# Tying a quad's differences to an earlier low part, and moving layer A's probability products one sub-block on

## The chip, the cores and the metric

The kernel runs on one core of one Trainium2 chip. The metric is the device time of one execution in microseconds (us). Five engines matter: PE (TensorE, matmuls), ACT (ScalarE), DVE (VectorE), POOL (GpSimd) and SP (SyncE, which here only issues transfers). Each works through its own queue in order, and they wait for each other through semaphores.

## The reference, cut to what matters

There are 256 tokens, a model width of 2048, an inner width of 4096, 32 heads of 128, one layer of each kind. All data are float32.

```python
h = rms_norm(x, a_norm)                                   # layer A
q, k, v, g = jnp.split(h @ a_w_in, 4, axis=-1)            # 2048 -> 4 * 4096
o = chunked_relbias_attention(q, k, v, a_rel_bias)        # softmax(q k^T * scale + bias) v, per head
x = x + (o * jax.nn.silu(g)) @ a_w_out                    # 4096 -> 2048
h_kv = rms_norm(x, kv_norm)                               # shared keys and values
k_sh, v_sh = jnp.split(h_kv @ kv_w, 2, axis=-1)
h = rms_norm(x, b_norm)                                   # layer B
q, g = jnp.split(h @ b_w_in, 2, axis=-1)
o = forgetting_attention(q, k_sh, v_sh, cum_log_f)        # softmax with a decay per key, causal
x = x + (o * jax.nn.silu(g)) @ b_w_out
return rms_norm(x, final_norm)
```

## The kernel before, in words

**Products.** A float32 product is made of three matmuls of rounded parts: with x = xh + xl and w = hi + lo, the kernel adds xh·hi, xh·lo and xl·hi. The weights stream in. A *sub-block* is 256 rows by 512 columns of a weight matrix (512 KB); SP loads it into a `raw` tile (6 buffers), ACT copies it, rounded, into `hi`, and DVE subtracts `lo = raw - hi` (hi and lo: 4 buffers each). PE then runs 12 matmuls on it (2 blocks of 128 rows, 2 halves of the tokens, 3 parts), each 128x512. `Feed.prepare` issues a sub-block's hi and lo up to `DEPTH` ahead of PE; `feed.by_act` and `feed.by_dve` remember the last of each.

**Units and pairs.** Layer A works on pairs of heads, g = 0 to 15. A pair has two *units* of 512 columns: `aqk` (q and k) and `avg` (v and gate), 8 sub-blocks each, each unit with two accumulators in PSUM (`aqk_acc`, `avg_acc`, one for each half of the tokens). For g > 0 the last two sub-blocks of both units are done together as *quads*: a 2x2 block product with seven products where there were eight (21 matmuls where there were 24). The order on PE in such a pair is: aqk 0 to 5; avg 0, 1; first quad; avg 2; second quad; avg 3, 4, 5 (`QUADS_A = (1, 2)` are the places of the quads behind avg's sub-blocks).

**A quad's operands.** `Quad.split(i)` makes four pairs of hi and lo from the raw sub-blocks `one` (of aqk) and `two` (of avg). i = 0 takes `one` as it stands; i = 1 takes the differences `t` (two subtractions, lines 299 and 300, into a tile that is named `first` in layer A); i = 2 takes half of `two`; i = 3 takes `one` again, overwritten by two more differences (lines 308 and 309, which come behind i = 0). So the rows are: ACT `quad_hi` (L305), DVE `quad_lo` (L306), DVE `first` (L299, L300), DVE `aqk_raw<-...` (L308, L309).

**Attention beside it.** The attention of the pair before runs as a generator (`side_a`, `attention`), whose steps are taken at places of the pair by tables: `A1_STEPS` counts behind aqk's sub-blocks, `A2_STEPS` behind avg's. Its steps: evacuate q and k (`qk`, L726, which also frees `aqk_acc`), transpose them on DVE (L519, into `first`) and through 16 small transfers into `sums` (8 on SP, 8 on POOL, L522); split them (`wide`, `q`); scores (`s1p`, `s0p` on PE); softmax; transpose the probabilities and the gate (`sgY` to `sgZ`, again 16 small transfers); split the probabilities (`wide<-sgZ`); multiply them with v (`op` on PE: six matmuls by `dot3`, L549 to L551, and two in plain float32, L613); then `oT` (L617). In the table before, the products `op` are issued behind avg 4.

**Order on the engines.** The program is written in one order; a scheduler then sets each engine's queue by what it expects to be ready. `tc.issue_after(ins)` holds what a block issues behind `ins` on the same engine.

**Output projection.** After layer A, `project(oA, ao, ...)` runs four units `ao0` to `ao3` over 16 sub-blocks with quads of their own (`ao_quads.order(first, second, n, lead)`: `lead` sub-blocks come ahead of the first quad), and the attention of pair 15 beside them by a list of counts. Layer B's pairs have one quad each; its output projection `bo` has five.

Of the kernel before, what the change touches and what calls it, by code (L numbers as in the profile page):

```python
# [30 lines left out]
KD = D // P  # L31
# [5 lines left out]
KB = 2  # L37
# [15 lines left out]
QUADS = 5  # L53
# [3 lines left out]
QUADS_A = (1, 2)  # L57
QUADS_B = (2,)
A1_STEPS = {3: 1, 4: 2}
A2_STEPS = {0: 1, 3: 1, 4: 99}  # L60
B1_STEPS = {3: 1, 5: 1, 6: 2}
B2_STEPS = {1: 1}
OLD_B_STEPS = {0: 1, 2: 99}
# [3 lines left out]
def r32(ap):  # L67
    return ap.bitcast(F32)
# [8 lines left out]
def trunk(ctx, tc, x, x_t, gains, a_w_in, a_rel, a_w_out, kv_w, f_w, f_b, b_w_in, b_w_out, final_norm, out):  # L77
    nc = tc.nc
    pe, act, dve, pool, sp = nc.tensor, nc.scalar, nc.vector, nc.gpsimd, nc.sync
# [50 lines left out]
    class Stat:  # L130
        def __init__(self, name, n):
            self.hi = [big_tile([P, BIG, S], F32R, name=f"{name}h{i}") for i in range(n // BIG)]
            self.lo = [big_tile([P, BIG, S], F32R, name=f"{name}l{i}") for i in range(n // BIG)]
# [55 lines left out]
    class Feed:  # L189
# [3 lines left out]
        def __init__(self, todo):  # L193
            self.todo = iter(todo)
            self.ready, self.loaded = [], []
            self.also, self.early = {}, []

        def buffer(self, name):
            return self.early.pop(0) if self.early else stream.tile([P, KB, IL, HN], F32, name=name, tag="raw",
# [21 lines left out]
        def prepare(self, ahead=True, parts=(slice(None),)):  # L221
            if not self.loaded:
                self.begin()
            if not self.loaded:
                return
            spec, b, raw, (before, behind) = self.loaded.pop(0)
            if not spec:
                self.ready.append(b[0].split(b[1]))
                self.refill()
                return  # L230
            if before:
                before()
            nm, h = spec["name"], b - (spec["nk"] // KB - spec["late"])
            if 0 <= h < spec["kept"]:
                both = big_tile([P, 2, KB, IL, HN], F32R, f"{nm}_keep{b}")
                hi, lo = both[:, 0], both[:, 1]
            else:
                hi = stream.tile([P, KB, IL, HN], F32R, name=f"{nm}_hi{b}", tag="hi", bufs=SPLIT)
                lo = stream.tile([P, KB, IL, HN], F32R, name=f"{nm}_lo{b}", tag="lo", bufs=SPLIT)
            if spec["g0"] is not None:  # L240
                for j in range(KB):
                    gk = gain[:, spec["g0"] + b * KB + j:][:, :1]
                    self.by_act = act.activation(hi[:, j], raw[:, j], AF.Copy, scale=gk)  # L243
                    self.by_dve = dve.scalar_tensor_tensor(lo[:, j], raw[:, j], gk, r32(hi[:, j]),  # L244
                                                           op0=OP.mult, op1=OP.subtract)
                parts = ()
            for j in parts:
                self.by_act = act.activation(hi[:, j], raw[:, j], AF.Copy)  # L248
                self.by_dve = dve.tensor_sub(lo[:, j], raw[:, j], r32(hi[:, j]))  # L249
            if behind:  # L250
                behind()
            self.ready.append((hi, lo))
            if ahead:
                self.refill()
# [26 lines left out]

    class Quad:

        def __init__(self, all_, specs, b, first, last):
            self.all, self.specs, self.b, self.first, self.last = all_, specs, b, first, last

        def split(self, i):

            one, two = self.raw
            t = self.all.t[:, 0]  # L290
            if not i:
                if self.specs[0]["g0"] is not None:
                    with tc.issue_after(feed.by_act.ins):
                        for raw, sp_ in zip(self.raw, self.specs):
                            for j in range(KB):
                                gk = gain[:, sp_["g0"] + self.b * KB + j:][:, :1]
                                act.activation(raw[:, j], raw[:, j], AF.Copy, scale=gk)
                with tc.issue_after(feed.by_dve.ins):
                    dve.tensor_sub(t[:, 0], two[:, 0], one[:, 0])  # L299
                    dve.tensor_sub(t[:, 1], two[:, 1], two[:, 0])  # L300
            src = [one, t, two[:, 1:], one][i]
            n = src.shape[1]
            hi = stream.tile([P, KB, IL, HN], F32R, name=f"quad_hi{i}", tag="hi", bufs=SPLIT)
            lo = stream.tile([P, KB, IL, HN], F32R, name=f"quad_lo{i}", tag="lo", bufs=SPLIT)
            feed.by_act = act.activation(hi[:, :n], src, AF.Copy)  # L305
            feed.by_dve = dve.tensor_sub(lo[:, :n], src, r32(hi[:, :n]))  # L306
            if not i:
                dve.tensor_sub(one[:, 0], two[:, 1], t[:, 0])  # L308
                dve.tensor_sub(one[:, 1], one[:, 1], one[:, 0])  # L309
            return hi, lo  # L310

        def step(self, lhs, first, second):
# [102 lines left out]
    a_quads = Quads("a")  # L415

    def paired(specs, places):

        n = len(places)
        quads = [Quad(a_quads, specs, KD // KB - n + i, not i, i == n - 1) for i in range(n)]  # L420
        todo.extend(whole(specs[0]))
        for i, item in enumerate(whole(specs[1])):
            todo.append(item)
            todo.extend((None, quads[k]) for k in range(n) if places[k] == i)
        return quads

    a_pairs = [paired(qkvg[2 * g:2 * g + 2], QUADS_A) for g in range(1, NG)]
    ao = [spec(f"ao{u}", a_w_out[u], KI) for u in range(4)]
    ao_quads, bo_quads = Quads("ao"), Quads("bo")
    ao_order = ao_quads.order(ao[0], ao[1], 3, 13) + ao_quads.order(ao[2], ao[3], QUADS, 4)  # L430
    todo += ao_order
    for g in range(NG):
        qkvg.append(spec(f"bqg{g}", b_w_in[g], KD, g0=GB, quads=len(QUADS_B) * (g > 0)))
# [8 lines left out]
    feed = Feed(todo)  # L442
# [36 lines left out]
    def project(lhs, specs, order, begun, closed, sides):  # L479


        units = {}

        def get(u):
            if u not in units:
                units[u] = Unit(lhs, specs[u])
            return units[u]

        for sp_, b in order:
            if sp_:  # L490
                us = [int(sp_["name"][-1])]
                get(us[0]).step(b)
            else:
                us = [int(u["name"][-1]) for u in b.specs]
                b.step(lhs, *(get(u) for u in us))
            for u in us:
                begun(u, units[u].left)
            for side, steps in sides:
                if steps:
                    steps[0] -= 1  # L500
                    while steps and steps[0] <= 0:
                        next(side, None)
                        steps.pop(0)
            for u in us:
                if not units[u].left:
                    more = closed(u, units[u].acc)
                    if more:
                        sides.append(more)
        for side, _ in sides:
            finish(side)  # L510
# [340 lines left out]
                           accum_out=ssq1[:, t, u:u + 1])  # L851
        return more and (more, [8, 7, 1, 1, 1] if u % 2 else [11, 1, 1, 1])

    project(oA, ao, ao_order, ao_begun, ao_closed, [(prev, [4, 1, 0, 1, 4, 1, 1]), (ao_quads.open(oA, QUADS), [3, 1, 1, 2, 26])])
    tot1 = const.tile([P, NT], F32, name="tot1")
    dve.tensor_reduce(tot1, ssq1, axis=AX.X, op=OP.add)
    rsB, halfB = rstd_of(tot1, "b")
# [236 lines left out]
```

## Time and profile before

| | |
|---|---|
| median of 3 runs | 1755.87 us (1755.2 to 1756.09) |
| the profiled execution's own time | 1756.25 us |
| its span | 1754.5 us |
| PE, DVE, ACT, POOL busy | 1721.5, 1560.7, 1200.3, 300.7 us |
| DMA, mean | 226 GB/s |

The span is what lies between the first and the last instruction; the rest of the execution's time, 1.75 us, lies around it. "Busy" counts an instruction's whole duration. PE's matmuls overlap: one of 128x512 lasts 0.38 us in the records, and the next may start long before it ends. So the time that PE loses at a wait is read from the starts of its matmuls, not from the idle time in a row.

A row of the timeline is: start in us, duration in us, engine, line, operation, output<-inputs, shape, and in brackets the idle time before it and what ended that.

### The profile page before, as it was taken

To read this page: it belongs to the slowest core of one execution; us is meant where nothing else is said; L and a number is where in the kernel's file an instruction comes from. 1 tells how busy PE (TensorE), PEld (TensorE's weight loads), DVE (VectorE), ACT (ScalarE), POOL (GpSimd) and SP (SyncE) were. 2 spreads that over 40 slices of the span, in tenths; PEclk is the share of its full clock that TensorE was granted. 3 is DMA by queue.
4 is the path that set the end of the run, shared out by engine and by line. 5 is a ranking of instruction groups with operands and counts; after the bars stand their busy time and mean duration, and the time that the engine had idled before them with its cause. 6 is when DMAs were issued, how large, how long until landed. Compare 5 with 4: busy or idle time off the path is not lost.

```text
span 1754.5 us, 27007 instructions
## 1 busy us (share of the span) xinstructions
PE 1721.5 (98%) x8213; PEld 1499.6 (85%) x8213; DVE 1560.7 (89%) x2378; ACT 1200.3 (68%) x2115; POOL 300.7 (17%) x623
## 2 busy tenths in 40 slices
PE   9999999999999999999999999999999999999997
PEld 7888888888888888888888888888888888888886
DVE  8799999999989999988977999999999989997887
ACT  7666666666656666655567777778788878775554
POOL 1011111111111111101121222212222122221000
PEclk9999999999999999999999999999999999999999
DMA  8666666666666666667775666666666666767654
GB/s 305 210 223 223 222 224 213 226 224 221 222 202 232 216 230 223 227 219 236 253 235 182 227 228 230 231 235 231 227 236 234 236 229 224 253 227 259 226 195 144
DMA packets 150321, 396.44 MB, mean 226 GB/s; under 512 B 31104, under 2 KB 51872, under 8 KB 150048
## 3 DMA queue, kind: packets, MB, share of 16 engines
q1 hardware_dynamic: 131536, 373.16, 61.1%
q0 software_dynamic: 17920, 20.48, 4.5%
q8 instruction: 66, 1.08, 0.3%
q10 hardware_dynamic: 720, 1.07, 0.2%
q14 instruction: 79, 0.65, 0.1%
HBM read 351.05 MB, written 4.23 MB: 202 GB/s over the span
## 4 chain that ended last, share of the span: by engine, by line
PE 84%; DVE 6%; DMA 5%; issue 2%; ACT 2%; SPq 0%; ACTq 0%; POOL 0%; DVEq 0%
PE bkv_acc L185 17%; PE bqg_acc L185 17%; PE aqk_acc L185 13%; PE avg_acc L185 9%; PE bo_acc L185 8%; PE ao_acc L185 6%; PE p L550 2%; PE p L551 2%; PE p L549 2%; DVE avg_lo L249 2%; DMA aqk_raw<-in_a_w_in 2%; DMA avg_raw<-in_a_w_in 1%; ACT quad_hi L305 1%; PE op L613 1%; DVE quad_lo L306 1%
## 5 line engine op out<-in xcount | busy, mean ns | idle before, releaser
L522 POOL DMA_DIRECT2D sums<-first x256 | 125.8, 499 | 563.0 <-ACT aqk_hi L248 254.4
L243 ACT ACTIVATE bqg_hi<-bqg_raw,gain 128x512 fp32r<-128x512 f32 x226 | 149.5, 713 | 85.4 <-DMA bqg_raw<-in_b_w_in 33.7
L244 DVE SCALAR_TENSOR_TENSOR bkv_lo<-bkv_raw,gain,bkv_hi 128x512 fp32r<-128x512 f32 x226 | 161.4, 761 | 16.4 <-ACT bkv_hi L243 16.2
L185 PE MATMUL bkv_acc<-bkv_hi,x1Th 128*128 128x512 f32 x452 | 167.7, 383 | 0.0
L185 PE MATMUL bqg_acc<-bqg_hi,x1Th 128*128 128x512 f32 x452 | 167.6, 382 | 0.0
L185 PE MATMUL bkv_acc<-bkv_hi,x1Tl 128*128 128x512 f32 x452 | 166.3, 380 | 0.0
L185 PE MATMUL bqg_acc<-bqg_hi,x1Tl 128*128 128x512 f32 x452 | 166.3, 380 | 0.0
L185 PE MATMUL bqg_acc<-bqg_lo,x1Th 128*128 128x512 f32 x452 | 166.3, 380 | 0.0
L185 PE MATMUL bkv_acc<-bkv_lo,x1Th 128*128 128x512 f32 x452 | 166.3, 380 | 0.0
L244 DVE SCALAR_TENSOR_TENSOR bqg_lo<-bqg_raw,gain,bqg_hi 128x512 fp32r<-128x512 f32 x226 | 156.4, 743 | 4.9 <-ACT bqg_hi L243 4.9
L243 ACT ACTIVATE bkv_hi<-bkv_raw,gain 128x512 fp32r<-128x512 f32 x226 | 145.1, 711 | 21.9 <-issue 14.7
L522 POOL DMA_DIRECT2D sgZ<-sgY x256 | 125.5, 498 | 155.1 <-PE avg_acc L185 80.1
L248 ACT ACTIVATE aqk_hi<-aqk_raw 128x1024 fp32r<-128x1024 f32 x95 | 100.3, 1056 | 70.6 <-PE avg_acc L185 47.4
L185 PE MATMUL aqk_acc<-aqk_hi,xTh 128*128 128x512 f32 x392 | 145.7, 385 | 0.0
L185 PE MATMUL avg_acc<-avg_hi,xTl 128*128 128x512 f32 x392 | 144.8, 383 | 0.0
L185 PE MATMUL aqk_acc<-aqk_lo,xTh 128*128 128x512 f32 x392 | 143.7, 380 | 1.0 <-DVE aqk_lo L249 1.0
L185 PE MATMUL avg_acc<-avg_lo,xTh 128*128 128x512 f32 x392 | 144.4, 382 | 0.0
L185 PE MATMUL aqk_acc<-aqk_hi,xTl 128*128 128x512 f32 x392 | 143.7, 380 | 0.0
L185 PE MATMUL avg_acc<-avg_hi,xTh 128*128 128x512 f32 x392 | 143.7, 380 | 0.0
L249 DVE TENSOR_TENSOR avg_lo<-avg_raw,avg_hi 128x1024 fp32r<-128x1024 f32 x97 | 115.9, 1222 | 11.7 <-ACT avg_hi L248 10.8
L248 ACT ACTIVATE avg_hi<-avg_raw 128x1024 fp32r<-128x1024 f32 x97 | 98.8, 1049 | 32.4 <-PE aqk_acc L185 28.0
L249 DVE TENSOR_TENSOR aqk_lo<-aqk_raw,aqk_hi 128x1024 fp32r<-128x1024 f32 x95 | 114.5, 1218 | 5.3 <-ACT aqk_hi L248 5.3
(373 smaller groups left out, 4614.0 us busy)
## 6 DMA issues: line engine op xcount, KB each, us to landing
bqg_raw<-in_b_w_in SPq DMA_DIRECT2D x128, 512.0 KB, 5.1
bkv_raw<-in_kv_w SPq DMA_DIRECT2D x128, 512.0 KB, 4.7
avg_raw<-in_a_w_in SPq DMA_DIRECT2D x127, 512.0 KB, 4.6
aqk_raw<-in_a_w_in SPq DMA_DIRECT2D x125, 512.0 KB, 5.3
ao_raw<-in_a_w_out SPq DMA_DIRECT2D x64, 512.0 KB, 4.5
bo_raw<-in_b_w_out SPq DMA_DIRECT2D x64, 512.0 KB, 4.3
sgZ<-sgY SPq DMA_DIRECT2D x256, 40.0 KB, 2.1
sgZ<-sgY POOLq DMA_DIRECT2D x256, 40.0 KB, 1.9
```

The costliest lines, as they stand in the source:

```text
L185: pe.matmul(acc[t], x[:, t * P:(t + 1) * P], w, start=t not in begun, stop=last and i == 2)
L243: self.by_act = act.activation(hi[:, j], raw[:, j], AF.Copy, scale=gk)
L244: self.by_dve = dve.scalar_tensor_tensor(lo[:, j], raw[:, j], gk, r32(hi[:, j]), op0=OP.mult, op1=OP.subtract)
L248: self.by_act = act.activation(hi[:, j], raw[:, j], AF.Copy)
L249: self.by_dve = dve.tensor_sub(lo[:, j], raw[:, j], r32(hi[:, j]))
L305: feed.by_act = act.activation(hi[:, :n], src, AF.Copy)
L306: feed.by_dve = dve.tensor_sub(lo[:, :n], src, r32(hi[:, :n]))
L522: queues[j].dma_start(out=r32(z)[j * SQ:(j + 1) * SQ, i], in_=y[i * SQ:(i + 1) * SQ, j])
L549: pe.matmul(out_, a[0], b[0], start=start, stop=False)
L550: pe.matmul(out_, a[0], b[1], start=False, stop=False)
L551: pe.matmul(out_, a[1], b[0], start=False, stop=stop)
L613: pe.matmul(op[:, i, 1::NT], v1[:, i * DH:(i + 1) * DH], pT[:, i, NT], start=False, stop=i == HG - 1)
```

## The change

Four things are edited.

1. Each low part is remembered in a list `lows`. The differences `t` of a quad (L299, L300) were held behind the latest low part; now they are held behind `lows[tie - 1]`. `tie` is 0 for first quads (and for all of ao, bo and layer B): the latest, as before. It is -2 for the second quad of a pair of layer A: the third last.
2. The low part of i = 1 is held behind the second overwriting difference (`self.ready`), in every quad.
3. `op` and what follows it is issued behind avg 5 instead of avg 4.
4. In the output projection, 14 sub-blocks instead of 13 come ahead of the first quad, and pair 15's `op` is issued one count later.

```diff
-A2_STEPS = {0: 1, 3: 1, 4: 99}
+A2_STEPS = {0: 1, 3: 1, 5: 99}
...
-            self.also, self.early = {}, []
+            self.also, self.early, self.lows = {}, [], []
...
                 self.by_dve = dve.tensor_sub(lo[:, j], raw[:, j], r32(hi[:, j]))
+            self.lows.append(self.by_dve)
...
-        def __init__(self, all_, specs, b, first, last):
+        def __init__(self, all_, specs, b, first, last, tie=0):
...
-                with tc.issue_after(feed.by_dve.ins):
+                with tc.issue_after(feed.lows[self.tie - 1].ins):
                     dve.tensor_sub(t[:, 0], two[:, 0], one[:, 0])
                     dve.tensor_sub(t[:, 1], two[:, 1], two[:, 0])
...
-            feed.by_dve = dve.tensor_sub(lo[:, :n], src, r32(hi[:, :n]))
+            with tc.issue_after(self.ready.ins) if i == 1 else nullcontext():
+                feed.by_dve = dve.tensor_sub(lo[:, :n], src, r32(hi[:, :n]))
+            feed.lows.append(feed.by_dve)
             if not i:
                 dve.tensor_sub(one[:, 0], two[:, 1], t[:, 0])
-                dve.tensor_sub(one[:, 1], one[:, 1], one[:, 0])
+                self.ready = dve.tensor_sub(one[:, 1], one[:, 1], one[:, 0])
...
-        quads = [Quad(a_quads, specs, KD // KB - n + i, not i, i == n - 1) for i in range(n)]
+        quads = [Quad(a_quads, specs, KD // KB - n + i, not i, i == n - 1, -2 * (i > 0)) for i in range(n)]
...
-    ao_order = ao_quads.order(ao[0], ao[1], 3, 13) + ao_quads.order(ao[2], ao[3], QUADS, 4)
+    ao_order = ao_quads.order(ao[0], ao[1], 3, 14) + ao_quads.order(ao[2], ao[3], QUADS, 4)
...
-    project(oA, ao, ao_order, ao_begun, ao_closed, [(prev, [4, 1, 0, 1, 4, 1, 1]), ...
+    project(oA, ao, ao_order, ao_begun, ao_closed, [(prev, [4, 1, 0, 1, 5, 1, 1]), ...
```

The change adds no instruction to PE, ACT or DVE and takes none away; it moves some. Three lines were added, so what was L549 is now L552, L613 is L616, L519 is L522, and so on.

**DVE at the second quad of a pair (pair 4).** Before, with `first1` the differences `t`, `aqk4_raw7` and `avg4_raw7` the second quad's raw sub-blocks, and numbers behind `quad_lo` for i:

```order
L306 TENSOR_TENSOR quad_lo2_2074<-avg4_raw6_1858,quad_hi2_2073 128x512
L306 TENSOR_TENSOR quad_lo3_2096<-aqk4_raw6_1856,quad_hi3_2095 128x1024
L249 TENSOR_TENSOR avg4_lo2_2108<-avg4_raw2_1909,avg4_hi2_2107 128x1024
L299 TENSOR_TENSOR first1_102<-avg4_raw7_1929,aqk4_raw7_1927 128x512
L300 TENSOR_TENSOR first1_102<-avg4_raw7_1929 128x512
L306 TENSOR_TENSOR quad_lo0_2122<-aqk4_raw7_1927,quad_hi0_2121 128x1024
L306 TENSOR_TENSOR quad_lo1_2131<-first1_102,quad_hi1_2130 128x1024
L308 TENSOR_TENSOR aqk4_raw7_1927<-avg4_raw7_1929,first1_102 128x512
L306 TENSOR_TENSOR quad_lo2_2141<-avg4_raw7_1929,quad_hi2_2140 128x512
L309 TENSOR_TENSOR aqk4_raw7_1927<-aqk4_raw7_1927 128x512
L306 TENSOR_TENSOR quad_lo3_2159<-aqk4_raw7_1927,quad_hi3_2158 128x1024
```

The same place now:

```order
L308 TENSOR_TENSOR quad_lo2_2074<-avg4_raw6_1844,quad_hi2_2073 128x512
L300 TENSOR_TENSOR first1_102<-avg4_raw7_1929,aqk4_raw7_1927 128x512
L301 TENSOR_TENSOR first1_102<-avg4_raw7_1929 128x512
L308 TENSOR_TENSOR quad_lo3_2096<-aqk4_raw6_1842,quad_hi3_2095 128x1024
L249 TENSOR_TENSOR avg4_lo2_2108<-avg4_raw2_1909,avg4_hi2_2107 128x1024
L308 TENSOR_TENSOR quad_lo0_2122<-aqk4_raw7_1927,quad_hi0_2121 128x1024
L311 TENSOR_TENSOR aqk4_raw7_1927<-avg4_raw7_1929,first1_102 128x512
L312 TENSOR_TENSOR aqk4_raw7_1927<-aqk4_raw7_1927 128x512
L308 TENSOR_TENSOR quad_lo1_2131<-first1_102,quad_hi1_2130 128x1024
L308 TENSOR_TENSOR quad_lo2_2141<-avg4_raw7_1929,quad_hi2_2140 128x512
L308 TENSOR_TENSOR quad_lo3_2159<-aqk4_raw7_1927,quad_hi3_2158 128x1024
```

The differences `t` of the second quad moved ahead of two low parts (the first quad's last and avg 2's), and both overwriting differences moved ahead of the low part of i = 1.

**The end of a pair (pair 5 into pair 6) on PE, and into pair 5 on DVE.** PE before, with `op` the probability products, `avg5_acc` the end of the unit and `aqk6_acc` the start of the next pair:

```order
L185 MATMUL avg5_acc0_2324<-avg5_lo5_2629,xTh1_106 128x512
L550 MATMUL op_2712<-wide_2689,vh_2311 128x256
L551 MATMUL op_2712<-wide_2689,vl_2312 128x256
L549 MATMUL op_2712<-wide_2689,vh_2311 128x256
L550 MATMUL op_2712<-wide_2689,vh_2311 128x256
L551 MATMUL op_2712<-wide_2689,vl_2312 128x256
L613 MATMUL op_2712<-sgZ_2492,v1_2313 128x128 x2
L185 MATMUL avg5_acc0_2324<-avg5_hi5_2628,xTl1_108 128x512
L185 MATMUL avg5_acc1_2325<-avg5_hi5_2628,xTh1_106 128x512
L185 MATMUL avg5_acc1_2325<-avg5_lo5_2629,xTh1_106 128x512
L185 MATMUL avg5_acc1_2325<-avg5_hi5_2628,xTl1_108 128x512
L185 MATMUL aqk6_acc0_2759<-aqk6_hi0_2671,xTh0_105 128x512
```

PE now:

```order
L185 MATMUL avg5_acc1_2325<-avg5_hi5_2628,xTl1_108 128x512
L552 MATMUL op_2732<-wide_2689,vh_2311 128x256
L553 MATMUL op_2732<-wide_2689,vh_2311 128x256
L554 MATMUL op_2732<-wide_2689,vl_2312 128x256
L552 MATMUL op_2732<-wide_2689,vh_2311 128x256
L553 MATMUL op_2732<-wide_2689,vh_2311 128x256
L554 MATMUL op_2732<-wide_2689,vl_2312 128x256
L616 MATMUL op_2732<-sgZ_2492,v1_2313 128x128 x2
L185 MATMUL aqk6_acc0_2759<-aqk6_hi0_2671,xTh0_105 128x512
```

`op` moved from inside avg 5 (four matmuls of that sub-block came behind it) to behind it, so that nothing lies between it and the next pair. DVE there before, from the low part of the next pair's second sub-block on:

```order
L249 TENSOR_TENSOR aqk5_lo1_2258<-aqk5_raw1_2144,aqk5_hi1_2257 128x1024
L726 SCALAR_TENSOR_TENSOR qk_2213<-aqk4_acc1_1886,rstd_a_393,comb_103 128x512
L617 TENSOR_TENSOR oT_2284<-op_2275,sgZ_2055 128x256
L519 STREAM_TRANSPOSE first1_102<-qk_2213 128x1024
L617 TENSOR_TENSOR oT_2284<-op_2275,sgZ_2055 128x256
L249 TENSOR_TENSOR aqk5_lo2_2290<-aqk5_raw2_2162,aqk5_hi2_2289 128x1024
```

DVE now:

```order
L249 TENSOR_TENSOR aqk5_lo1_2258<-aqk5_raw1_2144,aqk5_hi1_2257 128x1024
L729 SCALAR_TENSOR_TENSOR qk_2213<-aqk4_acc1_1886,rstd_a_393,comb_103 128x512
L249 TENSOR_TENSOR aqk5_lo2_2276<-aqk5_raw2_2162,aqk5_hi2_2275 128x1024
L522 STREAM_TRANSPOSE first1_102<-qk_2213 128x1024
L620 TENSOR_TENSOR oT_2304<-op_2295,sgZ_2055 128x256 x2
```

The transposition of q and k now stands behind one more low part, and on SP the load of one more raw sub-block stands ahead of the eight transfers of that transposition; `oT` stands behind both.

**PE in the output projection, where pair 15's `op` lies.** Before:

```order
L185 MATMUL ao0_acc1_7134<-ao0_hi14_7370,oAh3_187 128x512
L185 MATMUL ao0_acc1_7134<-ao0_lo14_7371,oAh3_187 128x512
L549 MATMUL op_7433<-wide_7408,vh_7116 128x256
L185 MATMUL ao0_acc1_7134<-ao0_hi14_7370,oAl3_191 128x512
L185 MATMUL ao1_acc0_7465<-ao1_hi3_7388,oAh0_184 128x512
```

Now:

```order
L185 MATMUL ao0_acc1_7134<-ao0_hi14_7370,oAl3_191 128x512
L185 MATMUL ao1_acc0_7462<-ao1_hi3_7388,oAh0_184 128x512
L185 MATMUL ao1_acc0_7462<-ao1_lo3_7389,oAh0_184 128x512
L552 MATMUL op_7453<-wide_7426,vh_7116 128x256
L185 MATMUL ao1_acc0_7462<-ao1_hi3_7388,oAl0_188 128x512
L185 MATMUL ao1_acc1_7463<-ao1_hi3_7388,oAh0_184 128x512
```

The scheduler had already put `op` later than its place in the program; it now comes three matmuls later than before, and one load of a raw sub-block more stands on SP ahead of the transfers of `sgZ`.

More of the change, by code (lines that the diff above doesn't have):

```diff
@@ L282, in trunk @@
     class Quad:
-        def __init__(self, all_, specs, b, first, last):
-            self.all, self.specs, self.b, self.first, self.last = all_, specs, b, first, last
+        def __init__(self, all_, specs, b, first, last, tie=0):
+            self.all, self.specs, self.b, self.first, self.last, self.tie = all_, specs, b, first, last, tie
         def split(self, i):
@@ L852, in ao_closed @@
         return more and (more, [8, 7, 1, 1, 1] if u % 2 else [11, 1, 1, 1])
-    project(oA, ao, ao_order, ao_begun, ao_closed, [(prev, [4, 1, 0, 1, 4, 1, 1]), (ao_quads.open(oA, QUADS), [3, 1, 1, 2, 26])])
+    project(oA, ao, ao_order, ao_begun, ao_closed, [(prev, [4, 1, 0, 1, 5, 1, 1]), (ao_quads.open(oA, QUADS), [3, 1, 1, 2, 26])])
     tot1 = const.tile([P, NT], F32, name="tot1")
```

## The prediction

> **What bounds the kernel now.** I began with the page's first part and the table of stretches, one pair of layer A to a stretch (columns: length, then busy time and instructions of PE, weight load, DVE, ACT and POOL, PE's clock, DMA share, GB/s).
>
> ```profile
> span 1754.5 us, 27007 instructions
> PE 1721.5 (98%) x8213; PEld 1499.6 (85%) x8213; DVE 1560.7 (89%) x2378; ACT 1200.3 (68%) x2115; POOL 300.7 (17%) x623
> ...
> 226.38:270.48 44.10, 43.19 (x207) 37.24 (x207) 40.86 (x58) 28.88 (x47) 8.01 (x17) 1.00 0.66 223
> 270.48:315.62 45.14, 43.44 (x207) 37.31 (x207) 40.77 (x58) 28.72 (x47) 8.04 (x17) 1.00 0.64 218
> 492.02:538.37 46.35, 44.15 (x207) 37.52 (x207) 40.76 (x58) 28.68 (x47) 8.03 (x17) 1.00 0.63 212
> ...
> 1037.98:1081.01 43.03, 43.03 (x211) 38.06 (x210) 39.62 (x68) 34.59 (x70) 9.07 (x18) 1.00 0.66 230
> ```
>
> PE is the bound. A pair of layer B (last row) has no idle time on PE at all. A pair of layer A has 44.10 - 43.19 = 0.91 us; of its 15 pairs with quads 13 last 44.10 us and two last 1.04 and 2.25 us more (rows two and three). So whatever the change can win lies in layer A's waits and a few single ones. The list of PE's waits names them (total, times, longest):
>
> ```profile
> PE aqk_acc L550 <- DVE quad_lo L306: 8.4, 15, 0.6
> PE op L549 <- ACT wide L541: 2.6, 1, 2.6
> PE op L613 <- DMA avg_raw<-in_a_w_in: 2.5, 7, 0.4
> ```
>
> The first is there once in each pair; the third, with the same wait under other releasers, too. What they cost is read from the starts of PE's matmuls. Back to back one starts 12.95/60 = 0.216 us after the other (first row, from the chain of waits). The rest is PE's timeline of one pair: its second quad begins at 255.17.
>
> ```profile
> 315.62 12.95 PE aqk_acc L185 x60
> ...
> 255.17 0.38 PE L549 MATMUL p<-quad_hi,xTh 128*128 128x512 f32 x1
> ...
> 258.20 0.38 PE L551 MATMUL avg_acc<-quad_hi,sums 128*128 128x512 f32 x1
> 258.56 0.48 PE L549 MATMUL aqk_acc<-quad_hi,xTh 128*128 128x512 f32 x1
> ...
> 259.82 0.48 PE L550 MATMUL aqk_acc<-quad_lo,xTh 128*128 128x512 f32 x1 [0.56 <-DVE quad_lo L306]
> ...
> 260.79 0.38 PE L185 MATMUL avg_acc<-avg_hi,xTh 128*128 128x512 f32 x1
> ...
> 268.30 0.28 PE L551 MATMUL op<-wide,vl 128*128 128x256 f32 x1
> 268.93 0.68 PE L613 MATMUL op<-sgZ,v 128*128 128x128 f32 x4 [0.35 <-DMA avg_raw<-in_a_w_in]
> ...
> 269.67 0.38 PE L185 MATMUL avg_acc<-avg_hi,xTh 128*128 128x512 f32 x1
> ...
> 270.31 0.60 PE L185 MATMUL aqk_acc<-aqk_hi,xTh 128*128 128x512 f32 x2
> ```
>
> From 258.20 to 260.79 lie seven steps: 1.51 us of work took 2.59, so the quad's wait costs **1.08 us**. The products `op` have a twin with the same shapes, the scores, where nothing waits:
>
> ```profile
> 239.72 0.28 PE L551 MATMUL s1p<-wide,q 128*128 128x256 f32 x1
> 239.83 0.61 PE L573 MATMUL s0p<-sums,q 128*128 128x128 f32 x4
> ...
> 240.50 0.38 PE L185 MATMUL aqk_acc<-aqk_lo,xTh 128*128 128x512 f32 x1
> ```
>
> Last of the six, four passes, two large matmuls: 0.78 us there, 269.67 - 268.30 = 1.37 at `op`. That wait costs **0.59 us**. Together 1.67 of a pair's 44.10.
>
> **Why PE waits at the quad, and what moving the differences does.** DVE and ACT in the same pair:
>
> ```profile
> 249.40 1.22 DVE L306 TENSOR_TENSOR quad_lo<-aqk_raw,quad_hi 128x1024 fp32r<-128x1024 f32 x1 [1.10 <-ACT quad_hi L305]
> ...
> 252.43 0.69 DVE L300 TENSOR_TENSOR first<-avg_raw 128x512 f32<-128x512 f32 x1
> ...
> 256.67 0.69 DVE L309 TENSOR_TENSOR aqk_raw<-aqk_raw 128x512 f32<-128x512 f32 x1
> 258.54 1.23 DVE L306 TENSOR_TENSOR quad_lo<-aqk_raw,quad_hi 128x1024 fp32r<-128x1024 f32 x1 [1.18 <-ACT quad_hi L305]
> 259.68 3.49 DVE L249 TENSOR_TENSOR avg_lo<-avg_raw,avg_hi 128x1024 fp32r<-128x1024 f32 x3
> ...
> 267.27 0.76 DVE L542 TENSOR_TENSOR wide<-sgZ,wide 128x256 fp32r<-128x256 f32 x2
> ...
> 269.07 0.75 DVE L726 SCALAR_TENSOR_TENSOR qk<-aqk_acc,rstd_a,comb 128x512 f32<-128x512 f32 x1
> ...
> 270.06 1.24 DVE L519 STREAM_TRANSPOSE first<-qk 128x1024 f32<-128x1024 f32 x1
> ...
> 256.02 0.60 ACT L348 ACTIVATE comb<-p 128x512 f32<-128x512 f32 x1 [1.21 <-PE p L551]
> 257.45 1.06 ACT L305 ACTIVATE quad_hi<-aqk_raw 128x1024 fp32r<-128x1024 f32 x1 [0.83 <-DVE aqk_raw L309]
> ```
>
> The chain of the stall: L309 ends at 257.4, ACT's hi of i = 3 starts then, DVE's low part behind it, and PE, which wants it at 258.63 (16 steps behind 255.17), gets it at 259.8. Meanwhile DVE sat idle twice for over a microsecond, at 249.40 and 258.54. In the new order the two differences `t` (1.2 us) fill the first of these gaps, and both overwriting differences come ahead of the low part of i = 1. By the same durations: `t` 248.3 (249.40 less the idle 1.10) to 249.5, the first quad's last low part to 250.6 (as now), avg 2's to 251.9, i = 0's to 253.1, L308 and L309 to **254.3** instead of 257.4. ACT's hi of i = 3 then waits for its buffer alone, which avg 2 frees when PE leaves it (255.4): 255.4 to 256.4. DVE's low parts of i = 1 and 2 end at 256.0, that of i = 3 at **257.7**, 0.9 us ahead of PE. The low parts that were pushed back keep their time: i = 1's, at 255.4, is wanted at 256.7 (seven steps behind 255.17). All 1.08 us go.
>
> **What stands behind it.** From 259.68 to 269.73 DVE works without a break (three low parts, combining the products, `wide`, both evacuations `qk`). Its start moves to 258.0, when ACT, behind the hi of i = 3 and the copy at L348 (0.5 to the next start), has avg 3's hi; so `wide` is split at 266.3 and the second `qk` done at 268.1.
>
> **`op`.** At the end of avg 5 PE arrives, without both waits, at 259.71 + 36 steps = 267.5, 1.2 us behind the split. In today's order the six matmuls are themselves held by DVE (267.27) and nothing runs ahead while PE's queue works off what stands before L613; in the new order they are not held, as the scores are not, so I price `op` like them: 0.59 us go. A pair becomes 44.10 - 1.67 = **42.43 us**. PE's floor is met by DVE with little to spare: 40.86 busy.
>
> **What comes later for it.** With nothing behind `op`, the next pair begins at 268.5 and writes its second accumulator at 268.7; the `qk` that frees it ends at 268.1. That is 0.6 us, the smallest margin. And q and k's transposition, behind one more low part (1.1 us), ends at 270.4, 1.9 us into the next pair, where now it ends 1.0 us in: 0.95 later for its transfers. The extra load ahead of them on SP is issued while DVE transposes, and costs nothing by itself. In an ordinary pair nothing waits for these transfers; in the two long ones, and in the output projection, ACT does, where POOL's issue breaks off:
>
> ```profile
> 235.20 0.40 ACT L541 ACTIVATE wide<-sums 128x256 fp32r<-128x256 f32 x1
> ...
> 276.04 1.48 POOL L522 DMA_DIRECT2D sums<-first  x3 [1.65 <-issue]
> ...
> 281.94 0.42 ACT L541 ACTIVATE wide<-sums 128x256 fp32r<-128x256 f32 x1 [2.55 <-DMA avg_raw<-in_a_w_in]
> ```
>
> POOL's queue is unchanged, so I let these breaks stand and charge 0.95 us more at each of the three places.
>
> **Output projection.** Its `op` waits once, 2.56 us, and PE's clock falls:
>
> ```profile
> 750.62 0.58 PE L549 MATMUL op<-wide,vh 128*128 128x256 f32 x1 [2.56 <-ACT wide L541]
> ...
> 751.00:752.00 1.00, 1.00 (x4) 0.82 (x4) 0.96 (x3) 0.28 (x1) 0.00 (x0) 0.50 1.01 414
> ...
> 842.88 0.38 PE L549 MATMUL ao_acc<-quad_hi,oAh 128*128 128x512 f32 x1
> 843.96 0.48 PE L550 MATMUL ao_acc<-quad_lo,oAh 128*128 128x512 f32 x1 [0.70 <-DVE quad_lo L306]
> ...
> 1715.98 0.48 PE L550 MATMUL bo_acc<-quad_lo,oBh 128*128 128x512 f32 x1 [0.67 <-DVE quad_lo L306]
> ```
>
> PE arrives there three matmuls later, so the wait shrinks by 0.65 us; the transfers it waits for follow the scores, which move with PE. Bounds: the wait grows by 1.1 (one low part more ahead of `sgY`), or goes with its slow clock. Half a clock for some three microseconds costs about 1.5 us; I keep it. The Trainium skill, "TensorE: Matmul & The Clock Gate", Part 1 and "Why this matters for your kernels", has the clock halved after an idle window of about 3.4 us and advises gaps under about 3. Here 2.56 us was enough, so the measured row decides; by the rule a wait of 1.9 us would leave the clock full, and the sum would be 1.5 us better. The other edit to `split` removes waits like the one at 843.96 (1.08 where a step is 0.22, and 0.1 behind it: 0.97 us), where L309 stood last too; layer B's final projection has one of the same size (1715.98). Together 1.9. Layer B's pairs have no wait to lose; their order on DVE does not change.
>
> **The sum.** 13 x 1.67 = 21.7; two long pairs 2 x (1.67 - 0.95) = 1.4; output projection -0.95 + 0.65; late quads 1.9. That is 24.7 us off 1756.25, the profiled execution's own time, or 1731.5. The median of the runs is 0.4 lower: **1731 us**, 1.4% faster. Differences under about 0.2% cannot be told from none here.
>
> **Rivals.**
>
> *The accumulator's margin does not hold (half the gain).* If DVE is 0.6 to 1.4 us later at `qk` than I work out, PE waits at the head of each pair instead: 0.8 us of 1.67 come back, 15 x 0.8 = 12, about 1743. For it: DVE works without a break for 10 us ahead of `qk`, and 40.86 of 42.43 us in all. Against it: its idle time stands ahead of that stretch and absorbs delays.
>
> *DVE is the bound already (no change).* If its 3.2 idle microseconds a pair (44.10 - 40.86) persist, the pair stays at 44.10 and the time within 2 us of 1756. For it: 93% busy. Against it: 1.10 and 1.18 of them are waits for ACT that the order makes, as shown.
>
> *The late transposition holds the scores in every pair (slower).* ACT starts the split for the scores 235.20 - 226.4 = 8.8 us into a pair; at 281.94 it was 11.6, and that pair lost 1.04 us in all. So a delay of about 2 us is free. If q and k's transfers landed so much later in each pair, behind the 512 KB load on their queue, that it looked like the one of 46.35, a pair would be 2.25 + 0.95 - 1.67 = 1.5 us longer, 15 times: 1779. It decides from a delay of about 3.5 us on. For it: the transposition is 0.95 later, and the load is new there. Against it: 0.95 is half of what is free.
>
> *The breaks vanish and the clock stays full (better).* The two long pairs' 1.04 and 2.25, 1.9 of the charges, and the clock's 1.5 add up to 6.7: 1725.
>
> **Chances.** 0.62 for the forecast with its own range of 1727 to 1736; 0.16 for half the gain; 0.06 for better; 0.08 for no change; 0.08 for slower. From 1725.5 to 1745 lies 0.8. Faster by over 0.2%: 0.84; within: 0.08; slower: 0.08.
>
> **What would show it.** Right: ordinary pairs of 42.4 us with PE idle near zero; no wait of `aqk_acc` for `quad_lo`; `op` without a wait; ACT's hi of i = 3 no longer released by L312; DVE over 96% busy in a pair. Wrong: a new wait at the first `aqk_acc` matmul of a pair for `qk` (first rival), DVE's waits for `quad_hi` unchanged (second), the scores waiting for `sums` in each pair (third).

## The result, and the profile after

| | before | after | predicted |
|---|---|---|---|
| median of 4 runs | 1755.98 us | 1734.46 us (1732.83 to 1735.95) | 1731 (1725.5 to 1745) |
| ratio | | 0.9877, 95% interval 0.9860 to 0.9894 | 0.986 |
| profiled execution, its span | 1756.25, 1754.5 us | 1732.83, 1731.1 us | 1731.5 |

The change saves 21.5 us by the medians and 23.4 us between the two profiled executions; 24.7 were predicted. The changed kernel's four runs are two near 1733 and two near 1736, and the profiled one is of the lower kind.

The page's first part, after:

```profile
span 1731.1 us, 26983 instructions
...
PE 1710.2 (99%) x8213; PEld 1498.4 (87%) x8213; DVE 1561.4 (90%) x2378; ACT 1195.1 (69%) x2115; POOL 301.0 (17%) x623
```

PE's and DVE's work is the same, in a span that is 23 us shorter. The table of stretches answers to the one of before (columns as there): an ordinary pair (pair 5), and the two long ones (6 and 11, in which q and k of pairs 5 and 10 are transferred).

```profile
220.26:262.64 42.38, 42.38 (x207) 37.39 (x207) 40.78 (x58) 28.46 (x48) 8.04 (x17) 1.00 0.69 232
262.64:308.10 45.46, 43.59 (x207) 37.59 (x207) 40.78 (x58) 28.21 (x48) 8.04 (x17) 1.00 0.64 216
477.62:520.97 43.35, 42.64 (x207) 37.30 (x207) 40.77 (x58) 28.28 (x48) 8.05 (x17) 1.00 0.66 227
```

An ordinary pair lasts 42.38 us (42.43 predicted, 44.10 before), PE is never idle in it, and DVE is busy for 40.78 of it, 96%. Of the long pairs one is longer than before (45.46 against 45.14), the other shorter (43.35 against 46.35).

The timeline of that ordinary pair, PE first, then DVE and ACT:

```profile
249.06 0.38 PE L552 MATMUL p<-quad_hi,xTh 128*128 128x512 f32 x1
...
252.51 0.38 PE L553 MATMUL aqk_acc<-quad_lo,xTh 128*128 128x512 f32 x1
...
253.59 0.38 PE L185 MATMUL avg_acc<-avg_hi,xTh 128*128 128x512 f32 x1
...
261.92 0.28 PE L554 MATMUL op<-wide,vl 128*128 128x256 f32 x1
262.03 0.61 PE L616 MATMUL op<-sgZ,v 128*128 128x128 f32 x4
262.39 0.68 PE L185 MATMUL aqk_acc<-aqk_hi,xTh 128*128 128x512 f32 x2
...
242.95 0.68 DVE L301 TENSOR_TENSOR first<-avg_raw 128x512 f32<-128x512 f32 x1
...
247.80 0.69 DVE L312 TENSOR_TENSOR aqk_raw<-aqk_raw 128x512 f32<-128x512 f32 x1
...
250.40 1.23 DVE L308 TENSOR_TENSOR quad_lo<-aqk_raw,quad_hi 128x1024 fp32r<-128x1024 f32 x1 [0.17 <-ACT quad_hi L306]
...
261.23 0.74 DVE L729 SCALAR_TENSOR_TENSOR qk<-aqk_acc,rstd_a,comb 128x512 f32<-128x512 f32 x1
...
249.31 1.06 ACT L306 ACTIVATE quad_hi<-aqk_raw 128x1024 fp32r<-128x1024 f32 x1 [2.01 <-PE avg_acc L185]
```

The low part of i = 3 starts at 250.40, and PE takes it at 252.51 without a wait (21 steps from 249.06 to 253.59 at 0.216 us). ACT's hi of i = 3 is released by PE, which frees its buffer, no longer by L312. Between the last of the six products and the next pair lie 0.47 us, and L616 has no wait in its bracket. The evacuation `qk` that frees the accumulator ends at 261.97, 0.6 us before the next pair's second accumulator is written.

The chain of waits gives the starts of the regions, before and then after (pair 1, pair 15, layer B):

```profile
49.98 12.95 PE aqk_acc L185 x60
...
670.67 12.95 PE aqk_acc L185 x60
...
894.10 12.95 PE bqg_acc L185 x60
```

```profile
49.95 12.95 PE aqk_acc L185 x60
...
648.20 12.95 PE aqk_acc L185 x60
...
871.07 12.95 PE bqg_acc L185 x60
```

With 44.10 and 42.38 us for pair 15, the pairs shrink from 664.8 to 640.6 us (24.2 less), the output projection with what follows it grows from 179.3 to 180.5 (1.2 more), and the rest shrinks by 0.4. That is the 23.4 us. The loss in the projection shows in PE's waits and in its timeline there:

```profile
PE op L552 <- ACT wide L544: 4.2, 1, 4.2
PE aqk_acc L553 <- DVE quad_lo L308: 1.7, 3, 0.8
...
PE p L553 <- DVE quad_lo L308: 0.6, 1, 0.6
```

```profile
718.72 1.51 DVE L522 STREAM_TRANSPOSE sgY<-sg 128x1280 f32<-128x1280 f32 x1
...
728.88 0.72 ACT L544 ACTIVATE wide<-sgZ 128x256 fp32r<-128x256 f32 x2 [5.12 <-DMA sgZ<-sgY]
...
703.98 0.38 PE L552 MATMUL s1p<-wide,q 128*128 128x256 f32 x1 [0.45 <-ACT q L544]
...
729.35 0.58 PE L552 MATMUL op<-wide,vh 128*128 128x256 f32 x1 [4.25 <-ACT wide L544]
```

Pair 15's `op` waited 2.56 us before and 4.25 us now, and PE now waits 0.45 us for the operands of pair 15's scores (`s1p`), for which it did not wait before. The quads' wait, 15 times before, is left in three pairs: pair 2 (0.20 us) and the two long ones (0.81 and 0.71 us).

### The profile page after: what moved, and what is told of

Read it like the earlier page. It is cut to its first block, busy times and chain, and to the rows that moved or that the text cites. A ratio compares the mean times of both kernels' runs of the same rounds, so it can differ in the third digit from the quotient of the medians.

```text
span 1731.1 us, 26983 instructions
## 1 busy us (share of the span) xinstructions
PE 1710.2 (99%) x8213; PEld 1498.4 (87%) x8213; DVE 1561.4 (90%) x2378; ACT 1195.1 (69%) x2115; POOL 301.0 (17%) x623
## 3 DMA queue, kind: packets, MB, share of 16 engines
q8 instruction: 66, 1.08, 0.3%
## 4 chain that ended last, share of the span: by engine, by line
PE 93%; DVE 3%; DMA 1%; ACT 1%; issue 1%; POOL 0%; SPq 0%; ACTq 0%; DVEq 0%
PE bkv_acc L185 17%; PE bqg_acc L185 17%; PE avg_acc L185 14%; PE aqk_acc L185 13%; PE bo_acc L185 8%; PE ao_acc L185 6%; PE p L553 3%; PE p L554 3%; PE p L552 3%; PE op L616 1%; PE aqk_acc L553 1%; PE s0p L576 1%; PE aqk_acc L554 1%; PE aqk_acc L552 1%; DVE quad_lo L308 1%
## 5 line engine op out<-in xcount | busy, mean ns | idle before, releaser
L185 PE MATMUL bkv_acc<-bkv_hi,x1Th 128*128 128x512 f32 x452 | 167.5, 382 | 0.0
```

The source lines that it names most:

```text
L185: pe.matmul(acc[t], x[:, t * P:(t + 1) * P], w, start=t not in begun, stop=last and i == 2)
```

## The experiments

They came in three groups, with the kernel before timed beside each: 1757.25, 1757.67 and 1756.49 us. Ratios are to that. The length of a pair is read from the starts of successive `op` (L613, L616).

### Are the quad's wait and op's wait two losses? Four kernels that undo or keep single edits

`quads_only`: before with edits 1 and 2 (shown against the changed kernel: edits 3 and 4 undone).

```diff
-A2_STEPS = {0: 1, 3: 1, 5: 99}
+A2_STEPS = {0: 1, 3: 1, 4: 99}
...
-    ao_order = ao_quads.order(ao[0], ao[1], 3, 14) + ...
+    ao_order = ao_quads.order(ao[0], ao[1], 3, 13) + ...
...
-    project(..., [(prev, [4, 1, 0, 1, 5, 1, 1]), ...
+    project(..., [(prev, [4, 1, 0, 1, 4, 1, 1]), ...
```

> The kernel before with edits 1 and 2 alone (both orders at the quads); the products `op` stay where they were, the output projection's lead and count too. Theory: the quad's wait (1.08 us) and op's wait (0.59 us) are two separate losses, so an ordinary pair falls from 44.10 to 43.02 us, op's wait stays at about 0.6, and with the late quads of the two output projections (1 to 2 us) the time is 1756 - 15 x 1.08 - 1.4 = about 1738 us, three quarters of the whole change's gain. The two or three long pairs keep the excess they had before (1.0 and 2.3 us), since the transposition of q and k stands where it stood. Rival: the two waits are one slack, and PE, coming 1.08 us earlier, waits that much longer for the probabilities at op (their transfers don't move): pairs of 43.6 to 44.1 us, 1747 to 1756.

Measured: 1744.85 us, ratio 0.9928 (0.9916 to 0.9941). An ordinary pair lasted 43.24 us, between the two expectations: the quads alone won 0.86, not 1.08.

`op_only`: before with edit 3.

```diff
-A2_STEPS = {0: 1, 3: 1, 4: 99}
+A2_STEPS = {0: 1, 3: 1, 5: 99}
```

> The kernel before with edit 3 alone: op behind avg 5. This also moves the transposition of q and k behind one more low part. Theory: op's 0.59 us go in each pair (43.5), the quad's 1.08 stay, the long pairs and the output projection lose about 0.95 us each to the later transposition: 1756 - 15 x 0.59 + 3 x 0.95 = about 1750. Rival: without the quads' edits DVE ends the evacuation that frees the accumulator only about 0.2 us ahead of PE, the next pair's head waits for it, and the pair stays at 43.8 to 44.1: 1753 to 1758.

Measured: 1749.75 us, ratio 0.9958 (0.9945 to 0.9970), pairs of 43.55 us, as the theory had it; the accumulator's wait did not come.

`tie_only` and `ready_only`: before with edit 1 alone, and with edit 2 alone (shown against `quads_only`).

```diff
-            with tc.issue_after(self.ready.ins) if i == 1 else nullcontext():
+            with nullcontext():
```

> The kernel before with edit 1 alone: the differences t of a pair's second quad tied to the third last low part; the low part of i = 1 isn't held. Theory: the stall is set by when the last overwriting difference ends; t filling the first gap moves that from 257.4 to about 256.2 of the profile before, which brings the low part of i = 3 to 258.5 against PE's 258.63, so this edit alone takes nearly all of the 1.08 us: pairs of 43.0 to 43.2, about 1740 to 1742. Rival: the two edits share the gain, each taking about half: 43.6 and 1748.

```diff
-                with tc.issue_after(feed.lows[self.tie - 1].ins):
+                with tc.issue_after(feed.by_dve.ins):
```

> The kernel before with edit 2 alone: the low part of i = 1 held behind the second overwriting difference, t where it was. Theory: by the durations of the profile before the last overwriting difference ends two low parts (1.8 us) earlier, at 255.6, and the low part of i = 3 at 257.9, 0.7 us ahead of PE; so this edit alone takes all of the 1.08 us as well (pairs of 43.0), and the late quads of the output projections besides: about 1738, the same as both edits together. Rival: the gap on DVE at the first quad stays, the low part of i = 1 itself comes too late for PE, and half of the gain is left: 43.6, 1747.

Measured: 1754.55 us, 0.9985 (0.9976 to 0.9993), and 1752.04 us, 0.9971 (0.9959 to 0.9983). Pairs lasted 43.83 and 43.78 us: both theories and both rivals missed, each edit won only some 0.3 us. PE's waits say why, first with edit 1, then with edit 2:

```profile
PE op L553 <- DVE wide L545: 8.2, 15, 0.8
...
PE aqk_acc L553 <- DVE quad_lo L308: 2.1, 4, 0.8
```

```profile
PE op L553 <- DVE wide L545: 3.4, 15, 0.3
...
PE p L553 <- DVE quad_lo L308: 1.8, 3, 0.8
```

The quad's wait is gone, as worked out (15 became 4; with edit 2, three longer ones are left at the low part of i = 1, and in each pair two steps of 0.42 and 0.32 us there in place of 0.22, which is 0.3 us in all and too short for the list). But PE then came earlier to `op` and waited there, in each pair, for the split probabilities, a wait that the list of before does not name. DVE's work behind the quad had not become early: one idle stretch of 1.2 or 1.1 us for ACT was left on it, and `wide` stands at its end.

The trace shows how firmly `op` is tied to `wide`. Ahead of L613 PE's queue holds eight instructions that wait for the 16 transfers of `sgZ` (0.05 us each, one about every 0.1 us). For one `op` of the kernel before, at 268.93:

```profile
L613 PEldq EVENT_SEMAPHORE  x8: 51/51/51, 268.1 to 268.8; - x8
```

They begin just when DVE has split `wide` (267.27 + 0.76 = 268.03), which the third of the six products ahead of them (268.08) waits for. So the wait at L613, whose row in the list names a raw load, is a wait for DVE as well. In all four kernels with `op` behind avg 4 (before, `quads_only`, `tie_only`, `ready_only`), L613 or L616 starts 0.90 to 1.00 us after the end of `wide`, in each of the 15 pairs. A pair of theirs is therefore as long as DVE takes from one `wide` to the next, to within 0.1 us. In the changed kernel the eight instructions stand from 260.2 to 261.1 beside the large matmuls of avg 5, and L616 starts 1.85 us after `wide` in an ordinary pair: the tie is gone.

### The other half of the table

`without_ready` and `without_tie`: the changed kernel with the same two lines undone.

> The changed kernel with edit 2 undone (edits 1, 3 and 4 stay). In the run with edit 1 alone PE's wait at the quad was gone but PE waited 0.53 us a pair at op for DVE's wide, and the pair was 43.83 us. Theory: a pair is as long as the longer of PE's work (42.38) and DVE's work with the idle time that its order makes; with op behind avg 5, PE no longer has to meet wide early, and DVE's 40.8 busy + 1.2 idle at the low part of i = 3 + 0.3 = 42.3 still fits: pairs of 42.4 to 42.6, time within 3 us of the whole change, 1735 to 1738. Rival: each edit at the quads is needed for its share, the accumulator's margin is used up and the next pair's head waits for qk: 43.1 to 43.3, about 1746.

> The changed kernel with edit 1 undone (edits 2, 3 and 4 stay). Theory: DVE's 40.8 busy + 1.1 idle at the first quad's last low part + 0.3 = 42.2 fits under PE's 42.38, so pairs of 42.4 to 42.6 (0.2 of it a wait for the low part of i = 1, seen in the run with edit 2 alone), 1734 to 1738. Rival: as above, 43.2, about 1746.

Measured: 1741.02 us, 0.9905 (0.9890 to 0.9919), and 1737.43 us, 0.9885 (0.9870 to 0.9899). Length of an ordinary pair in all eight combinations, us:

| edits at the quads | op behind avg 4 | op behind avg 5 |
|---|---|---|
| none | 44.10 | 43.55 |
| tie (1) | 43.83 | 42.44, in four pairs 43.0 to 43.5 |
| ready (2) | 43.78 | 42.69 |
| both | 43.24 | 42.38 |

The theory of 42.4 to 42.6 us holds for ordinary pairs with edit 1; with edit 2 they are 0.1 us above it. The times hold for `without_tie` (1734 to 1738 expected), but `without_ready` came out 3 us above the 1735 to 1738 expected, the four odd pairs adding 3.6 us to it. The rival (43.1 to 43.3) falls for edit 2 and holds only in some pairs for edit 1. Once `op` no longer asks for `wide` early, one of the quads' edits brings nearly all, because DVE's work and its remaining idle time fit under PE's 42.38. With both, the odd pairs go too but for one (pair 2, 43.17), and so does edit 2's 0.3 us, its wait at the low part of i = 1. The gains are not a sum: 0.86 for the quads and 0.55 for `op` make 1.41, together they are 1.72.

### What made the output projection longer?

`ao_as_before`: the changed kernel with edit 4 undone.

```diff
-    ao_order = ao_quads.order(ao[0], ao[1], 3, 14) + ...
+    ao_order = ao_quads.order(ao[0], ao[1], 3, 13) + ...
...
-    project(..., [(prev, [4, 1, 0, 1, 5, 1, 1]), ...
+    project(..., [(prev, [4, 1, 0, 1, 4, 1, 1]), ...
```

> The changed kernel with edit 4 undone: 13 sub-blocks ahead of the output projection's first quad, op at the count of before. Theory: the longer wait of pair 15's op (2.6 before, 4.25 after) comes with edit 2, since in the runs with edits 1 and 2, and with edit 2 alone, which have the old lead and count, it was 4.2 and 4.6 and the transposition of probabilities and gate stood behind one more low part and one more load there; so edit 4 is worth little: 180.5 to 181 us for the projection (180.5 after, 179.3 before), time within 0.7 us of the whole change. Rival: edit 4 brought the loss and undoing it gives 1.2 us or more back: 179.3, 1733.

Measured: 1735.83 us, 0.9876 (0.9859 to 0.9892), the same as the whole change. `op` waited 4.27 us. So edit 4 made neither the gain nor the loss. Over all kernels, op's wait was 4.58, 4.19, 4.27, 4.25 and 3.35 us where edit 2 was in (`ready_only`, `quads_only`, `ao_as_before`, after, `without_tie`; 4.9 and 3.8 in `half_scratch` and `turn_first` below), and 2.56, 2.74, 3.74 and 2.32 where it was not (before, `op_only`, `tie_only`, `without_ready`). In the first group the order has 12 of the projection's low parts ahead of the transposition `sgY`, and one more 512 KB load on SP ahead of its transfers; in the second it has 11. From the start of `sgY` to ACT's `wide` it took 10.16 us after, 9.13 before (741.02 to 750.15); over the first group 9.22 to 11.80, over the second 9.11 to 9.68. The groups nearly separate, so I take edit 2's order for the main cause; `tie_only` (3.74, with `op` three matmuls earlier on PE) shows that it is not the only thing that moves this wait.

`op_two_later`:

```diff
-    project(..., [(prev, [4, 1, 0, 1, 5, 1, 1]), ...
+    project(..., [(prev, [4, 1, 0, 1, 7, 1, 1]), ...
```

> The changed kernel with pair 15's op two counts later in the output projection (7 instead of 5: 20 matmuls later on PE, right ahead of the first quad). Theory: 20 x 0.216 = 4.3 us of work fill the 4.25 us wait, the clock doesn't fall (about 1.5 us), less up to 1.5 us if the first quad's products wait for the PSUM bank that op holds: 4 to 6 us less, 1729 to 1731. Rival: the quad's products wait for that bank, which oT frees late, as long as op waited before: no gain.

Measured: 1728.56 us, 0.9834 (0.9820 to 0.9849). The theory holds: from layer A's last `op` to layer B's first products it took 167.5 us instead of the changed kernel's 172.3, 4.8 less. The stretches around `op` show PE's clock (the column ahead of the DMA share), first of the changed kernel, then with `op` two later:

```profile
728.00:729.00 1.00, 0.00 (x0) 0.00 (x0) 0.00 (x0) 0.12 (x1) 0.00 (x0) 0.99 0.96 369
729.00:730.00 1.00, 0.65 (x2) 0.65 (x3) 0.67 (x2) 1.00 (x3) 0.00 (x0) 0.50 0.98 393
...
732.00:733.00 1.00, 1.00 (x7) 0.95 (x6) 0.34 (x2) 0.00 (x0) 0.38 (x2) 0.80 0.16 59
```

```profile
731.00:732.00 1.00, 0.77 (x4) 0.34 (x3) 0.64 (x2) 1.00 (x3) 0.00 (x0) 1.00 1.04 422
732.00:733.00 1.00, 0.67 (x5) 0.48 (x6) 0.81 (x2) 1.00 (x2) 0.32 (x3) 1.00 0.96 324
```

Without the wait the clock stays at 1.00.

### What makes the long pairs?

`half_scratch`: the changed kernel with half the memory for POOL's transfers.

```diff
-SCRATCH = 4096
+SCRATCH = 2048
```

> The changed kernel with half the memory that is set aside for POOL's transfers (SCRATCH 2048 instead of 4096). Nothing else changes. POOL's transfers stopped for 1.65 to 1.9 us after every 78 (in pairs 5, 10 and at pair 15's transfers). Theory: the stop comes when that memory has been used up once around, so it now comes after every 39, in six places of layer A instead of three, and those of them that fall on q and k's transfers make a long pair (1 to 3 us over 42.4): two to four long pairs, 1736 to 1741. Rival: the stops have another cause (they fall together with something in the program); they stay where they are, and the time stays at 1733 to 1736.

Measured: 1728.14 us, 0.9840 (0.9826 to 0.9853): faster, against both expectations. Layer A has no pair over 43.2 us left. POOL's transfers at the changed kernel's second stop, then at one of the stops with half the memory:

```profile
479.88 1.47 POOL L525 DMA_DIRECT2D sums<-first  x3 [18.83 <-DVE oT L620]
483.11 2.45 POOL L525 DMA_DIRECT2D sums<-first  x5 [1.76 <-issue]
```

```profile
435.10 1.47 POOL L525 DMA_DIRECT2D sums<-first  x3 [18.84 <-DVE oT L620]
437.33 2.44 POOL L525 DMA_DIRECT2D sums<-first  x5 [0.76 <-issue]
```

The stops came after every 35 transfers (twice after 70) instead of 78, so it is that memory that makes them. But they were also shorter, 0.60 to 0.88 us instead of 1.56 to 1.88, and that a pair hides.

`turn_first` and `turn_first_op_later`: the low part of aqk 2 held behind q and k's transposition, alone and with `op` two later.

```diff
-            self.also, self.early, self.lows = {}, [], []
+            self.also, self.early, self.lows, self.turned = {}, [], [], None
...
+            held = self.turned if nm.startswith("aqk") and b == 2 else None
             for j in parts:
                 self.by_act = act.activation(hi[:, j], raw[:, j], AF.Copy)
-                self.by_dve = dve.tensor_sub(lo[:, j], raw[:, j], r32(hi[:, j]))
+                with tc.issue_after(held.ins) if held else nullcontext():
+                    self.by_dve = dve.tensor_sub(lo[:, j], raw[:, j], r32(hi[:, j]))
...
-        dve.transpose(y, src.rearrange("p n (j u) -> p j n u", u=SQ))
+        turned = dve.transpose(y, src.rearrange("p n (j u) -> p j n u", u=SQ))
+        if name == "qk":
+            feed.turned = turned
```

> The changed kernel with one more hold: the low part of aqk's sub-block 2 behind the transposition of q and k, which thereby stands ahead of it on DVE again, as before the change, and on SP its eight transfers ahead of that raw load. Theory: the two long pairs (45.5 and 43.4 to 45.2 us after) lose the 1.1 us that the transposition is earlier, ordinary pairs stay at 42.4, the scores in the output projection come 1 us earlier: 2 to 4 us less, 1731 to 1732.5. Rival: the low part that is now later makes PE wait near the head of each pair (0.2 us or more, 15 times): 1738 or more.

> The changed kernel with that hold, and with pair 15's op two counts later. Theory: both gains add up (6 for op, 2 to 4 for the transposition): 1725 to 1727. Rival: the hold costs as much in the ordinary pairs as it wins in the long ones: 1728 to 1734.

Measured: 1734.91 us, 0.9878 (0.9864 to 0.9891), and 1728.86 us, 0.9843 (0.9829 to 0.9856): no gain over the kernels without the hold, and ordinary pairs stayed at 42.38. The hold moved the transposition by only 0.1 to 0.5 us, since an addition (`comb<-avg_acc`) took the free place on DVE. Pair 6 lost 0.5 and 0.9 us (44.95 and 44.54 against 45.46), but pair 11 lasted 45.84 and 45.74. So this test does not tell what the delay of the transposition costs. Pair 11 varies without any change in layer A: 43.36, 43.87 and 45.17 us in the changed kernel, `ao_as_before` and `op_two_later`. What sets it there is when the last transfers land, which the runs do not explain.

`turn_first_op_later_more_scratch`: the last one with `SCRATCH = 4608`.

> The last one with 4608 instead of 4096 set aside for POOL's transfers. Theory of the memory: a stop comes after every 88 instead of 78 transfers (16 to a pair), so in layer A they move from q and k's transfers to places of probabilities and gate or to other pairs, and one falls behind layer A: the long pairs of before vanish or stand elsewhere, time within 4 us of the last one in either direction. Rival (stops have another cause): the same stops at the same transfers and the same time.

Measured: 1722.33 us, 0.9808 (0.9795 to 0.9822), the fastest of all. The stops came after every 88 transfers and lasted about as long as with 4096:

```profile
517.80 3.42 POOL L529 DMA_DIRECT2D sums<-first  x7 [18.44 <-DVE first L524]
523.00 0.50 POOL L529 DMA_DIRECT2D sums<-first  x1 [1.78 <-issue]
```

Pairs 6 and 11 are ordinary now (42.38), the one at 517.80 (pair 12) is the only long one (44.95), and pair 15's transfers have no stop, which makes the stretch behind layer A another 3 us shorter. Both runs together show that the stops make the long pairs: they move, shrink and vanish with them.

## Why the prediction was right, and where not

**The ordinary pair (42.43 predicted, 42.38 measured).** The size was right, the picture behind it only half. I priced two separate waits, 1.08 and 0.59. Their sum holds for the whole change. But each alone brings less (0.86 and 0.55), and each quad edit alone 0.3, because both were waits for DVE: a pair is as long as the pass of DVE, its idle time included, wherever PE has to meet DVE inside the pair. The prediction saw that DVE holds the six products, but not that the wait at L613 behind them hangs on DVE too, so that PE loses there again what it wins at the quad. The chain from L312 to the low part of i = 3 was worked out rightly: 254.3 less the pair's start at 226.38 is 27.9 us into the pair, and L312 now ends 28.2 us in (248.49 less 220.26).

**The accumulator's margin** was put at 0.6 us and is 0.6. One reading beside it was 0.1 us off: 281.94 lies 11.5 us into its pair, not 11.6, and nothing hangs on that. The first rival (half the gain) and the second (DVE is the bound already) fell; the third (scores wait in each pair) too: in an ordinary pair PE waits for no scores. ACT does wait for `sums` in some (0.41 us at 229.59 in pair 5), and PE loses nothing by it.

**The two long pairs (1.4 us of gain predicted, 2.7 measured).** The prediction let POOL's stops stand and charged 0.95 us at each. Pair 6 came out 1.1 us longer than that (45.46 against 44.4), pair 11 2.2 us shorter (43.35 against 45.6). The stops did stand, the size did not hold, and pair 11 differs by 1.8 us between executions of the same layer A. That spread is of the size that divides the four runs; the runs that were not profiled cannot show whether it is its cause.

**The output projection (0.3 us lost there, without its late quad, was predicted; 2.1 were).** This step failed. I let op's wait shrink by 0.65 us since PE comes three matmuls later, and named one more low part ahead of `sgY` only as a bound (1.1 more). That low part did move ahead of `sgY`, and the wait grew by 1.69 us, 0.6 above that bound. From `sgY` to `wide` it took 1.03 us longer, with one more load ahead of the transfers; that this load is the reason is not shown. The 0.95 us charged for the late scores came out as 0.45. The clock's cost was kept in the sum, and it stayed: half speed again, for 3.4 us.

**Late quads (1.9 predicted).** The one in the output projection is gone from the list of waits. Of the one in layer B's projection 0.4 us at most came back, over all that follows layer A's projection: PE now waits 0.6 us there for the low part of i = 1, which edit 2 holds (`p<-quad_lo` in the waits), instead of 0.67 for i = 3.

So 24.2 - 1.2 + 0.4 = 23.4 us against 24.7. That the total is so near is partly luck: the pairs won 1.0 us more than the 23.1 predicted, and the output projection with its late quad came out 1.8 us worse, layer B 0.5 us worse. The rival that ended better needed the stops to vanish and the clock to stay full, and the change did neither. `op_two_later` kept the clock full, the two runs with another size of POOL's memory took away most of the long pairs, and the last kernel, which has both, is below that rival's 1725.

## What to carry to other kernels

Two waits of PE on the same second engine can be largely one loss: remove one and see whether PE meets that engine again further on, and try the edits in a two-by-two table before adding their prices. An edit that holds one instruction lets a scheduler reorder places far from it, so the order of every stage is worth reading, above all where a single wait also costs the clock. Stops at regular counts of transfers point to a buffer of the issuing engine; its size is worth a run, also a smaller one.

## What the runs showed of the hardware that I had not expected

POOL stops issuing after 35, 78 or 88 transfers with 2048, 4096 or 4608 set aside, for 0.60 to 0.88, 1.56 to 1.88 and 1.76 to 1.82 us. The Trainium skill, "DMA: Bandwidth & Descriptors", section "SWDGE vs HWDGE vs iDMA", says that transfers issued from GpSimd have their descriptors written by software into rings in SBUF. That fits a stop when the ring has been used up, though it states no such stop.

In `without_ready` PE's clock halved after an idle time of only 2.32 us, and it did so when PE had been working again for a microsecond. There `op` starts at 734.39 behind that wait:

```profile
734.00:735.00 1.00, 0.53 (x2) 0.34 (x3) 0.63 (x2) 1.00 (x3) 0.00 (x0) 1.00 0.96 381
735.00:736.00 1.00, 0.79 (x5) 0.50 (x5) 0.96 (x3) 0.59 (x1) 0.29 (x2) 0.71 1.06 410
736.00:737.00 1.00, 0.97 (x5) 1.00 (x5) 1.00 (x2) 0.00 (x0) 0.61 (x2) 0.50 0.96 393
737.00:738.00 1.00, 1.00 (x5) 0.82 (x4) 1.00 (x3) 0.00 (x0) 0.00 (x0) 0.50 1.03 404
738.00:739.00 1.00, 1.00 (x5) 0.79 (x4) 0.35 (x2) 0.62 (x1) 0.00 (x0) 0.59 0.63 244
```

At half speed a slice shows 0.50, so the slow time is 0.58 + 1 + 1 + 0.82 = 3.4 us; in the changed kernel it is 3.4 us as well. But it is not always that. In `tie_only` the clock is low from 745.8 to 752.6, for 6.8 us:

```profile
745.00:746.00 1.00, 0.00 (x0) 0.00 (x0) 1.00 (x2) 0.00 (x0) 0.00 (x0) 0.90 0.58 135
...
752.00:753.00 1.00, 1.00 (x4) 0.79 (x4) 0.31 (x1) 0.63 (x1) 0.00 (x0) 0.69 0.94 246
```

The slow time was 3.4 us in five kernels (before, `op_only`, `without_ready`, after, `ao_as_before`) and 6.8 us in six (`quads_only`, `tie_only`, `ready_only`, `without_tie`, `half_scratch`, `turn_first`). In the five PE was idle for at most 0.37 us after the clock had fallen, in the six for 0.75 to 2.39 us. The wait's length alone does not tell: 4.27 us went with 3.4 (`ao_as_before`), 3.35 with 6.8 (`without_tie`). The Trainium skill, "TensorE: Matmul & The Clock Gate", Part 1, has the clock set by a free-running window of 3413 ns. The slow times agree with one and with two such windows; that a whole idle window is needed does not agree with 2.32 us.
